# Order at the entry of a two-layer transformer kernel, the place of four small loads, and the last output tile in two halves

## The chip, the cores and the metric

The kernel runs on one core of a Trainium2 chip. The metric is the time of one execution on the device in microseconds (us). Five engines work side by side and wait for each other through semaphores: TensorE (PE in the profile, its weight loads as PEld), VectorE (DVE), ScalarE (ACT), GpSimd (POOL), and SyncE (SP), whose queue issues nearly all DMA transfers.

## The reference

The program computes a two-layer block over 512 latent tokens and 256 context tokens of width 1024. Each layer is an attention mixer and a SwiGLU feed-forward part; both take normalised tokens that are scaled and shifted by a modulation computed from a conditioning vector, and both are gated by it. Layer 0 mixes with windowed and dense grouped-query attention, layer 1 with differential attention, in which a scalar lambda weighs two softmaxes.

```python
s_c, s_cc = silu(c), silu(c_ctx)
for l in range(2):
    mx, mc = s_c @ mod_w[l] + mod_b[l], s_cc @ mod_w[l] + mod_b[l]
    shx1, scx1, gx1, shx2, scx2, gx2 = split(mx, 6)           # mc likewise
    hx = rms(x, norm_mix_w[l]) * (1 + scx1) + shx1            # hc likewise
    if l == 0:
        q, k, v (groups A and B) = hx @ ev_w_in, hc @ ev_w_in # then norms, rotary, attention
    else:
        lam = exp(sum(lq1 * lk1)) - exp(sum(lq2 * lk2)) + lam_init
        a = softmax(q1 k1) - lam * softmax(q2 k2)             # then values, norm, projection
    x = x + gx1 * mixed
    x = x + gx2 * (silu(gate) * up) @ ffn_w_out[l]            # gate, up from ffn_w_in[l]
    ...                                                       # ctx likewise in layer 0
return x
```

## The kernel before

Products that need full precision are made from halves: an operand is cast to a rounded float (`hi`) on ACT, the rest (`lo`) is subtracted on DVE or POOL, and three matmuls (hi by hi, hi by lo, lo by hi) add up in one PSUM bank.

**Entry.** Tokens lie in six tiles of 128 (four latent, two context, in the order `CTX_FIRST`). `start_mod(n)` makes two chunks of the modulation, shift (part 0) and scale (part 1), for 256 of the 1024 columns: `mod_steps` loads each chunk in two pieces of 512 KB (L177), multiplies them with the conditioning vector (L182), copies the row out of PSUM on ACT (`modr`, L185), turns it into columns with four small matmuls (`modcol`, L191), and `add_mod` adds the bias (L276) and, for the scale, the norm's weight (L280). Between these calls the tokens are normalised and transposed. Then, for each of the eight column blocks, DVE scales and shifts the transposed tokens (`xT`, L1165), ACT casts them (L1170) and DVE or POOL subtracts (L1171), into `hT` and `hTc`.

**First in-projection.** `weights0(0, ...)` loads the weights of the first head group in four pieces of 256 rows, three transfers each (`wir`, L493), casts each piece on ACT (`wihi`, L500) and subtracts on DVE (`wilo`, L501). The raw pieces share a ring of six buffers with the modulation's pieces (`start_tile`, tag `mw`), so a weight piece takes the buffer of a modulation piece that PE has used. In program order the loads of pieces 0 and 1 stand first, then the casts of 0 and 1, then the load and the cast of 2, then those of 3. `in_proj0` then sums 24 matmuls for each token tile (L466 to L468), two of the eight column blocks at a time.

**Order.** The program is traced in Python, and a planner orders each engine's queue by a simulated timeline: an instruction may move ahead of others that were written before it if its inputs are there sooner. From the sixth attention step on PE's own order is taken as written. `behind(name)` adds edges: what the block traces on the engine of the instruction kept in `turn[name]` is queued behind that instruction.

**Lambda.** `lambda_rows` makes four loads of 64 numbers each, one number per partition (L632). It is called in the second pass of layer 0's way out (`way_out0`), from the hook after the ninth hidden slice, `small_loads`. Its tile's pool is open from the start.

**Way out of layer 1.** `way_out1` holds eight PSUM banks, one for each pair of token tile and half row (512 columns). The last four hidden slices are held back: for one bank after the other, twelve matmuls finish the sum, `residual` multiplies by the gate (L473, in place in PSUM) and adds to the tokens (L474), and the 256 KB are stored (L1091).

Of the kernel before, what the change touches and what calls it, by code (L numbers as in the profile page):

```python
# [19 lines left out]
P = 128  # L20
# [9 lines left out]
NF = FFN // P  # L30
# [33 lines left out]
def backbone(es: ExitStack, tc: tile.TileContext, x, c, ctx, c_ctx, mod_w, mod_b, norm_mix_w, norm_ffn_w,  # L64
# [12 lines left out]
    turn = {"acc": 0, "tr": 0, "sum": 0}  # L77
# [12 lines left out]
    def raw_tile(shape, name):  # L90
        return keep.tile(shape, F32, name=name, tag="raw", bufs=2)
# [30 lines left out]
    start = Pool("start")  # L122
# [45 lines left out]
    def mod_steps(l, part, n, new_tile, pool, bank, wide=None, room=("modr", 1)):  # L168

        width, pieces = 256, 2  # L170
        c0 = part * D + n * width
        ps = p_1.tile([P, width], F32, name="mod", tag=bank) if wide is None else \
            wide.pool.tile([P, 1024], F32, name="mod", tag="sc", bufs=2)[:, :width]
        kp = KT // pieces
        for pc in range(pieces):
            w = new_tile([P, kp, width], "modw")
            nc.sync.dma_start(  # L177
                w, mod_w[l, pc * kp * P:(pc + 1) * kp * P, c0:c0 + width].rearrange("(j p) n -> p j n", p=P))
            for a in range(kp):
                k = pc * kp + a  # L180
                j = k % 4
                nc.tensor.matmul(ps[32 * j:32 * j + 32, :], s_pad[:, k, :], w[:, a, :],  # L182
                                 start=k < 4, stop=k >= 4, tile_position=(0, 32 * j))
        r = pool.tile([P, width], F32, name="modr", tag=room[0], bufs=room[1])
        nc.scalar.copy(r, ps)  # L185
        yield
        nb = width // P
        k0, k1 = n * nb, (n + 1) * nb
        pc2 = p_1.tile([P, nb, 2], F32, name="modcol", tag=bank)
        for b in range(nb):  # L190
            nc.tensor.matmul(pc2[:, b, :], r[:, b * P:(b + 1) * P], sel2, start=True, stop=True)  # L191
        add_mod(l, part, k0, k1, pc2, 2)
# [80 lines left out]
    def add_mod(l, part, k0, k1, ps, streams):  # L273

        mc = modc[l][:, part, k0:k1, 0:streams]
        nc.vector.tensor_tensor(mc, ps, bc(bcol[:, l, part, k0:k1], 2, streams), ALU.add)  # L276
        if part in (1, 4):
            f = 0 if part == 1 else 1
            w0 = 16 + 16 * f + 8 * l
            nc.vector.scalar_tensor_tensor(aff[l][:, f, k0:k1, 0:streams], mc, 1.0,  # L280
                                           bc(cols[:, w0 + k0:w0 + k1], 2, streams), ALU.add, ALU.mult)
# [198 lines left out]
        return hi, lo  # L480


    def weights0(b, wp, subs, new_tile=raw_tile):

        qc, kc, vc = ((b * 256, 512 + 64 * b, 640 + 64 * b) if b < 2 else
                      (768 + (b - 2) * 256, 1280 + 64 * (b - 2), 1408 + 64 * (b - 2)))
        for u in range(4):
            if u in (0, 2, 3):
                raws = []
                for v in ((0, 1), None, (2,), (3,))[u]:  # L490
                    raws.append(new_tile([P, 2, 384], "wir"))
                    for c0, c1, s in ((0, 256, qc), (256, 320, kc), (320, 384, vc)):
                        turn["load"] = nc.sync.dma_start(  # L493
                            raws[-1][:, :, c0:c1],
                            ev_w_in[0, v * 256:(v + 1) * 256, s:s + c1 - c0].rearrange("(j p) n -> p j n", p=P))
                if not u:
                    yield
            raw = raws.pop(0)
            hi, lo = (wp.tile([P, 2, 384], F32R, name=f"wi{z}", tag=f"w{z}", bufs=WBUF + 1) for z in ("hi", "lo"))
            nc.scalar.copy(hi, raw)  # L500
            subs[u % len(subs)].tensor_sub(lo, raw, f32(hi))  # L501
            yield hi, lo
# [125 lines left out]
    def lambda_rows(mp):  # L628

        lqk = mp.tile([HD, 4], F32, name="lqk")  # L630
        for j, a in enumerate((od_lq1, od_lk1, od_lq2, od_lk2)):
            nc.sync.dma_start(lqk[:, j:j + 1], a.rearrange("o d -> d o"))  # L632
        return lqk
# [415 lines left out]
    def way_out1(xs, hidr, pool, places_w, places_h):  # L1049

        banks = [p_1.tile([P, 512], F32, name="dps", tag=tag) for tag in ("tr0", "tr1", "acc0", "acc1")]
        banks += [singles.pool.tile([P, 512], F32, name="dps", tag=tag, bufs=2) for tag in ("p0", "p0", "p1", "p1")]
        places = [(t, n) for t in range(NTX) for n in range(2)]
        held = 4
        ready = {}

        def ready_hid(f):
            def views(raw):
                yield raw, ffn_w_out[1, f * P:(f + 1) * P, :]
            if f < len(places_w):  # L1060
                raw = raw_tile([P, D], "wdr")
                turn["load"] = nc.sync.dma_start(raw, ffn_w_out[1, f * P:(f + 1) * P, :])
                w, h = places_w[f], places_h[f]
                split_into(w, raw.rearrange("p (k c) -> p k c", k=4))
                split_into(h, hidr[f].rearrange("p (k c) -> p k c", k=2))
            else:
                w = [z.rearrange("p (k c) -> p k c", k=4) for z in unit(pool, views, [P, D], 5, "wd")]
                h = [pool.tile([P, 2, SEQ // 2], F32R, name=name, tag=name, bufs=5) for name in ("hdh", "hdl")]
                split_into(h, hidr[f].rearrange("p (k c) -> p k c", k=2))
            ready[f] = h, w  # L1070

        def sums(f, i):
            (t, n), ps = places[i], banks[i]
            hh, hl = (z[:, t // 2, t % 2 * P:(t % 2 + 1) * P] for z in ready[f][0])
            a, b = (z[:, 2 * n:2 * n + 2, :] for z in ready[f][1])
            nc.tensor.matmul(ps, hh, a, start=f == 0, stop=False)  # L1076
            nc.tensor.matmul(ps, hh, b, start=False, stop=False)  # L1077
            nc.tensor.matmul(ps, hl, a, start=False, stop=f == NF - 1)  # L1078

        g = gate_row(1, 5, 0, pool)  # L1080
        for f in range(NF - held):
            ready_hid(f)
            for i in range(len(places)):
                sums(f, i)
        for f in range(NF - held, NF):
            ready_hid(f)
        for i, (t, n) in enumerate(places):
            for f in range(NF - held, NF):
                sums(f, i)
            residual(xs[t], banks[i], g, n)  # L1090
            nc.sync.dma_start(out[0, t * P:(t + 1) * P, n * 512:(n + 1) * 512], xs[t][:, n * 512:(n + 1) * 512])  # L1091

    class Pairs:

# [50 lines left out]
    wp = Pool("mw0", "right")  # L1145
    xs = {t: load_x(t) for t in CTX_FIRST[:2]}
# [25 lines left out]


    mods = [(0, part, n) for part in (2, 3, 4) for n in range(4)]
    ws = list(weights0(0, wp.pool, (nc.vector,), start_tile))[1:]
    tabs = {}
    tables0(0, tabs, wp.pool)

# [66 lines left out]
    units = weights0(1, wp.pool, (nc.gpsimd, nc.vector))  # L1245
    next(units)
    ws = [next(units) for _ in range(2)]
    if True:
        for i, (b, t) in enumerate(steps):
            j = i % NT  # L1250
# [7 lines left out]
            if j == 4 and b < 2:  # L1258
                units = weights0(b + 2, wp.pool, (nc.gpsimd, nc.vector))
                next(units)  # L1260
            if b < 3:
                n = QUARTS[b][j]
# [13 lines left out]
                if j == 4 and b < 2:  # L1276
                    ws = [next(units) for _ in range(2)]
# [10 lines left out]
            if t == 0:  # L1288
# [13 lines left out]
                wp = Pool("w0", "right")  # L1302
                opa = Pool("opa", "right")
                xs = [None] * NT
                units = out_units0(wp.pool)
                ws = [next(units)]
# [36 lines left out]
        i = len(steps) - 1  # L1343
# [112 lines left out]
    if True:  # L1456
# [33 lines left out]
        places = [(rows[a], [z[:, a].rearrange("p (t c) -> p t c", c=P) for z in t2]) for a in range(4)]  # L1490
        raws = [f32(z)[:, 4 * half:5 * half].rearrange("p (t c) -> p t c", c=P) for z in rows4]
# [9 lines left out]
        ws1 = []  # L1501

        def small_loads():
            ws1.append(lambda_rows(cp))

        def early_weight(u):
            def room(shape, name):
# [13 lines left out]
    wp = Pool("mw1", "right")  # L1521
# [44 lines left out]
    if True:  # L1566
        new_head(ws1)
        first = state[0]
        banks = {t: acc_tile("inps") for t in CTX_FIRST[:2]}
# [34 lines left out]
        xs = xs1  # L1604
# [16 lines left out]
        ws, raws = [], []  # L1621
# [8 lines left out]
        for i in range(last - 1):  # L1630
# [14 lines left out]
            elif i in (23, 24):  # L1645
                z = keep.tile([P, 2, D], F32R, name="wo", tag=f"hTc{i - 23}")
# [37 lines left out]
        wp = Pool("w1", "right")  # L1684
# [203 lines left out]
```

## Time and profile before

| | |
|---|---|
| time, three runs | 1695.99 us median, 1693.12 to 1697.33 |
| profiled execution | 1692.5 us, span 1690.7 us |
| granted TensorE clock, mean | 0.995 |
| busy share of the span | PE 96%, PEld 87%, DVE 68%, ACT 56%, POOL 41% |
| HBM | 179.92 MB read, 12.87 MB written, 114 GB/s |

The span is the time from the first to the last instruction of the program; the execution's time has 1.8 us around it. A row of a timeline reads: start, length, engine, line of the kernel, operation, what it writes and reads, shapes, how many in a row, and in brackets the engine's idle time before it and what ended it. An engine name with a q is its sequencer: SPq rows are DMA issues. A row of a window table reads: stretch, length, busy time and count of PE, PEld, DVE, ACT and POOL, granted clock, share of the 16 DMA engines, GB/s. A row of waits reads: total, times, longest.

### The profile page before, as it was taken

Reading aid. Unit: us, or ns where it says so; the run is one execution under the profiler, and the core shown is the slowest. Engines: PE = TensorE matmul, PEld = TensorE weight load, DVE = VectorE, ACT = ScalarE, POOL = GpSimd, SP = SyncE. Lnnn points to the kernel's source line nnn. Section 1 sums busy time; section 2 is a strip of 40 time slices with the busy share of each in tenths; the row PEclk is TensorE's granted clock in tenths of the full one; section 3 lists DMA queues with packets and bytes.
Section 4 is the critical chain, followed back from the end, with each engine's and each line's share of the span. In section 5 each row is a group of like instructions: output and inputs, shape, how many; then the busy total and the mean of one; then the engine's idle time right before and its main releaser. Section 6 shows DMA issues by size and latency. Waiting matters only on the chain. (4 is left out here: it accounts for less than half of the span.)

```text
span 1690.7 us, 28553 instructions
## 1 busy us (share of the span) xinstructions
PE 1628.1 (96%) x10378; PEld 1465.3 (87%) x10378; DVE 1143.5 (68%) x2012; ACT 938.4 (56%) x2011; POOL 695.1 (41%) x867
## 2 busy tenths in 40 slices
PE   6999999899999999999999989999999999999998
PEld 3877777677999999998877889999988899999887
DVE  3765656754799887767767656666666598887433
ACT  5565555745456665544664456666666555555321
POOL 2665554321445554412413366666665242221000
PEclk9999999999999999999999999999999999999999
DMA  9222221411455555439966311111112433331431
GB/s 315 75 71 71 73 70 51 173 52 39 134 162 174 165 158 161 135 107 348 307 184 184 98 42 38 47 45 43 46 47 101 124 94 103 108 103 57 137 99 63
DMA packets 217964, 194.64 MB, mean 115 GB/s; under 512 B 20000, under 2 KB 202592, under 8 KB 217824
## 3 DMA queue, kind: packets, MB, share of 16 engines
q1 hardware_dynamic: 217472, 192.62, 36.9%
q8 instruction: 81, 1.33, 0.3%
q14 instruction: 59, 0.48, 0.1%
q10 hardware_dynamic: 352, 0.21, 0.0%
HBM read 179.92 MB, written 12.87 MB: 114 GB/s over the span
## 5 line engine op out<-in xcount | busy, mean ns | idle before, releaser
L901 ACT CAST wbh<-wr 128x512 fp32r<-128x512 f32 x170 | 104.9, 621 | 139.4 <-PE p L933 78.6
L933 PE MATMUL p<-hT,wbh 128*128 128x256 f32 (+1 forms) x752 | 154.4, 299 | 0.0
L911 POOL TENSOR_TENSOR wbl<-wr,wbh 128x512 fp32r<-128x512 f32 x43 | 60.2, 1400 | 174.2 <-ACT wbh L901 174.2
L933 PEld LDWEIGHTS p<-hT,wbh 128*128 128x128 f32 x752 | 121.9, 191 | 0.2
L911 DVE TENSOR_TENSOR wbl<-wr,wbh 128x512 fp32r<-128x512 f32 x127 | 106.4, 847 | 22.2 <-ACT wbh L901 17.8
L933 PE MATMUL p<-hT,wbl 128*128 128x256 f32 (+1 forms) x376 | 111.9, 298 | 0.0
L933 PE MATMUL p<-t,wbh 128*128 128x384 f32 (+1 forms) x480 | 111.3, 318 | 0.0
L604 POOL TENSOR_SCALAR Pt<-Pt,rc 128x256 f32<-128x256 f32 (+3 forms) x96 | 73.1, 772 | 86.9 <-DVE rc L601 79.6
L231 POOL TENSOR_TENSOR modp<-modp 128x512 f32<-128x512 f32 x40 | 57.3, 1433 | 116.5 <-ACT modp L230 116.5
L933 PE MATMUL p<-hTt,wbh 128*128 128x256 f32 (+1 forms) x480 | 101.0, 303 | 0.0
L466 PE MATMUL inps<-wih,hT 128*128 128x384 f32 x256 | 90.0, 351 | 7.2 <-ACT qkv L677 7.2
L887 POOL TENSOR_TENSOR wr<-wr 128x512 f32<-128x512 f32 x40 | 61.6, 1541 | 84.3 <-DVE ws L892 81.9
L933 PE MATMUL p<-b,wbh 128*128 128x384 f32 x368 | 93.8, 336 | 0.4 <-DVE c L961 0.4
L901 ACT CAST wbh<-ws 128x512 fp32r<-128x512 f32 x120 | 69.3, 579 | 42.1 <-PE p L933 31.0
L224 DVE SCALAR_TENSOR_TENSOR ma<-modw,cols,ma 128x256 f32<-128x256 f32 x140 | 87.0, 621 | 2.3
L592 ACT ACTIVATE Pt<-sc,nm 128x256 f32<-128x256 f32 (+3 forms) x96 | 67.8, 708 | 34.8 <-DVE nm L588 18.8
L468 PE MATMUL inps<-wih,hT 128*128 128x384 f32 x256 | 86.1, 336 | 0.0
L467 PE MATMUL inps<-wil,hT 128*128 128x384 f32 x256 | 86.0, 336 | 0.0
L911 DVE TENSOR_TENSOR wbl<-ws,wbh 128x512 fp32r<-128x512 f32 x120 | 81.8, 681 | 2.1 <-ACT wbh L901 2.0
L933 PEld LDWEIGHTS p<-t,wbh 128*128 128x128 f32 x480 | 82.9, 189 | 0.0
L933 PEld LDWEIGHTS p<-hTt,wbh 128*128 128x128 f32 x480 | 78.3, 191 | 3.1 <-ACT modp L230 2.1
L230 ACT ACTIVATE modp<-modw,cols 128x256 f32<-128x256 f32 x160 | 68.3, 499 | 17.1 <-POOL ma L236 8.6
(355 smaller groups left out, 5357.4 us busy)
## 6 DMA issues: line engine op xcount, KB each, us to landing
modw<-in_mod_w_dram SPq DMA_DIRECT2D x96, 512.0 KB, 4.4
wr<-in_ffn_w_in_dram SPq DMA_DIRECT2D x176, 256.0 KB, 3.1
wdr<-in_ffn_w_out_dram SPq DMA_DIRECT2D x66, 512.0 KB, 3.7
wir<-in_od_w_in_dram SPq DMA_DIRECT2D x96, 128.0 KB, 2.3
hidm<-hid SPq DMA_DIRECT2D x44, 192.0 KB, 1.9
hr<-hidm SPq DMA_DIRECT2D x22, 192.0 KB, 3.1
x<-in_x_dram SPq DMA_DIRECT2D x8, 512.0 KB, 6.2
wir<-in_ev_w_in_dram SPq DMA_DIRECT2D x16, 256.0 KB
```

The source lines that it names most:

```text
L224: nc.vector.scalar_tensor_tensor(acc, w[:, k], scale[k], acc, ALU.mult, ALU.add)
L230: nc.scalar.activation(pr[:, k], w[:, k], AF.Copy, scale=scale[k])
L231: nc.gpsimd.tensor_add(pr[:, 0:2], pr[:, 0:2], pr[:, 2:4])
L466: nc.tensor.matmul(ps, hs[0][:, k, :], a, start=k == 0, stop=False)
L467: nc.tensor.matmul(ps, hs[0][:, k, :], b, start=False, stop=False)
L468: nc.tensor.matmul(ps, hs[1][:, k, :], a, start=False, stop=k == KT - 1)
L592: turn["exp"] = nc.scalar.activation(p[:, :n], s, AF.Exp, bias=nm[:, c1], accum_out=sm[:, c1])
L604: nc.gpsimd.tensor_scalar(p[:, :n], p[:, :n], rc[:, hh:hh + 1], 1.0, ALU.mult, ALU.mult)
L887: nc.gpsimd.tensor_sub(w, raw[f, "G1"], w)
L901: nc.scalar.copy(hi, w)
L911: (nc.gpsimd if name == "G2" else nc.vector).tensor_sub(lo, raw[need[n]], f32(hi))
L933: nc.tensor.matmul(ps, w[:, k, :], H[b][h][:, k, :], start=first and k == 0 and q == 0, stop=final and k == 3 and q == 2, skip_group_check ...
```

## The change

- `mod_steps` keeps its latest row copy in `turn["modr"]`.
- `weights0` takes a list of which pieces are loaded at which step; the other callers keep the old one. The entry calls it so that all four pieces are loaded in the first step, and traces the four casts inside `behind("modr")`: on ACT they are queued behind the last row copy of `start_mod(3)`.
- `small_loads` traces the lambda loads inside `behind("load")`: on SP they are queued behind the weight load of the way out that was traced last.
- `way_out1` takes its last bank (token tile 3, columns 512 to 1023) in two halves of 256 columns: twelve matmuls, multiply, add and store for the first half, then the same for the second. Both halves are slices of the same PSUM bank.

```diff
         r = pool.tile([P, width], F32, name="modr", tag=room[0], bufs=room[1])
-        nc.scalar.copy(r, ps)
+        turn["modr"] = nc.scalar.copy(r, ps)
...
-    def weights0(b, wp, subs, new_tile=raw_tile):
+    def weights0(b, wp, subs, new_tile=raw_tile, loads=((0, 1), (), (2,), (3,))):
...
-            if u in (0, 2, 3):
+            if not u:
                 raws = []
-                for v in ((0, 1), None, (2,), (3,))[u]:
...
+            for v in loads[u]:
+                raws.append(new_tile([P, 2, 384], "wir"))
+                for c0, c1, s in ((0, 256, qc), (256, 320, kc), (320, 384, vc)):
+                    turn["load"] = nc.sync.dma_start(
...
+            if not u:
+                yield
...
-        for i, (t, n) in enumerate(places):
+        for i, (t, n) in enumerate(places[:-1]):
             for f in range(NF - held, NF):
                 sums(f, i)
             residual(xs[t], banks[i], g, n)
             nc.sync.dma_start(out[0, t * P:(t + 1) * P, n * 512:(n + 1) * 512], xs[t][:, n * 512:(n + 1) * 512])
+        t, n = places[-1]
+        for c in range(2):
+            ps, cs = banks[-1][:, c * 256:(c + 1) * 256], slice(n * 512 + c * 256, n * 512 + (c + 1) * 256)
+            for f in range(NF - held, NF):
+                hh, hl = (z[:, t // 2, t % 2 * P:(t % 2 + 1) * P] for z in ready[f][0])
+                a, b = (z[:, 2 * n + c, :] for z in ready[f][1])
+                nc.tensor.matmul(ps, hh, a, start=False, stop=False, skip_group_check=True)
+                nc.tensor.matmul(ps, hh, b, start=False, stop=False, skip_group_check=True)
+                nc.tensor.matmul(ps, hl, a, start=False, stop=f == NF - 1, skip_group_check=True)
+            nc.vector.tensor_mul(ps, ps, g[:, cs])
+            nc.vector.tensor_add(xs[t][:, cs], xs[t][:, cs], ps)
+            nc.sync.dma_start(out[0, t * P:(t + 1) * P, cs], xs[t][:, cs])
...
-    ws = list(weights0(0, wp.pool, (nc.vector,), start_tile))[1:]
+    units = weights0(0, wp.pool, (nc.vector,), start_tile, ((0, 1, 2, 3), (), (), ()))
+    next(units)
+    with behind("modr"):
+        ws = list(units)
...
         def small_loads():
-            ws1.append(lambda_rows(cp))
+            with behind("load"):
+                ws1.append(lambda_rows(cp))
```

More of the change, by code (lines that the diff above doesn't have):

```diff
@@ L487, in weights0 @@
         for u in range(4):
-            if u in (0, 2, 3):
+            if not u:
                 raws = []
-                for v in ((0, 1), None, (2,), (3,))[u]:
[L491 to L497, printed above, removed]
+            for v in loads[u]:
+                raws.append(new_tile([P, 2, 384], "wir"))
+                for c0, c1, s in ((0, 256, qc), (256, 320, kc), (320, 384, vc)):
+                    turn["load"] = nc.sync.dma_start(
+                        raws[-1][:, :, c0:c1],
+                        ev_w_in[0, v * 256:(v + 1) * 256, s:s + c1 - c0].rearrange("(j p) n -> p j n", p=P))
+            if not u:
+                yield
             raw = raws.pop(0)
@@ L1075, in sums @@
             a, b = (z[:, 2 * n:2 * n + 2, :] for z in ready[f][1])
-            nc.tensor.matmul(ps, hh, a, start=f == 0, stop=False)
-            nc.tensor.matmul(ps, hh, b, start=False, stop=False)
-            nc.tensor.matmul(ps, hl, a, start=False, stop=f == NF - 1)
+            nc.tensor.matmul(ps, hh, a, start=f == 0, stop=False, skip_group_check=True)
+            nc.tensor.matmul(ps, hh, b, start=False, stop=False, skip_group_check=True)
+            nc.tensor.matmul(ps, hl, a, start=False, stop=f == NF - 1, skip_group_check=True)
         g = gate_row(1, 5, 0, pool)
@@ L1091, in way_out1 @@
             nc.sync.dma_start(out[0, t * P:(t + 1) * P, n * 512:(n + 1) * 512], xs[t][:, n * 512:(n + 1) * 512])
+        t, n = places[-1]
[5 more added lines that the diff above has]
+                nc.tensor.matmul(ps, hh, a, start=False, stop=False, skip_group_check=True)
+                nc.tensor.matmul(ps, hh, b, start=False, stop=False, skip_group_check=True)
+                nc.tensor.matmul(ps, hl, a, start=False, stop=f == NF - 1, skip_group_check=True)
+            nc.vector.tensor_mul(ps, ps, g[:, cs])
+            nc.vector.tensor_add(xs[t][:, cs], xs[t][:, cs], ps)
+            nc.sync.dma_start(out[0, t * P:(t + 1) * P, cs], xs[t][:, cs])
     class Pairs:
```

## The prediction

> **What bounds the kernel now.** I read the page first, then the clock and transfer windows of the first 60 us, then the timelines of SP, ACT, DVE and PE there, and last the timeline of the final 8 us.
>
> ```profile
> span 1690.7 us, 28553 instructions
> PE 1628.1 (96%) x10378; PEld 1465.3 (87%) x10378; DVE 1143.5 (68%) x2012; ACT 938.4 (56%) x2011; POOL 695.1 (41%) x867
> ```
>
> TensorE is busy for 96% of the span, so only what PE does not do, or does at a lower clock, can be won. The change touches three places: the entry, up to the first in-projection sums; the second pass of layer 0's way out, where the lambda rows are now loaded; and the last output tile. SP's queue in the entry:
>
> ```profile
> 22.69 1.24 SPq L632 DMA_DIRECT2D lqk<-in_od_lq_dram  x1
> 25.95 0.47 SPq L632 DMA_DIRECT2D lqk<-in_od_lk_dram  x1
> 27.60 2.93 SPq L177 DMA_DIRECT2D modw<-in_mod_w_dram  x5
> ...
> 28.00:29.00 1.00, 1.00 (x10) 0.20 (x8) 0.07 (x1) 0.70 (x2) 0.00 (x0) 0.50 0.48 71
> 29.00:30.00 1.00, 1.00 (x8) 0.71 (x5) 0.00 (x0) 0.37 (x1) 0.00 (x0) 0.60 0.80 236
> ```
>
> The last three numbers of a window are granted clock, DMA share and GB/s. The four lambda loads, a few hundred bytes each, stand on SP between 22.69 and 26.42, ahead of the last five pieces of modulation weight. Two microseconds later the transfer engines run dry, the only two slices with a share under 0.9 between 3 and 40 us. Next ACT, the engine that makes the weights' casts and copies the modulation rows out of PSUM:
>
> ```profile
> 40.42 0.83 ACT L500 CAST wihi<-wir 128x768 fp32r<-128x768 f32 x1 [2.72 <-DMA wir<-in_ev_w_in_dram]
> 41.15 0.36 ACT L185 COPY modr<-mod 128x256 f32<-128x256 f32 x1
> 41.60 1.80 ACT L500 CAST wihi<-wir 128x768 fp32r<-128x768 f32 x2
> 44.33 0.36 ACT L185 COPY modr<-mod 128x256 f32<-128x256 f32 x1
> ```
>
> ACT stands idle for 2.72 us in front of a cast whose weights have not landed, with two row copies queued behind it. DVE does the same with the cast's low half:
>
> ```profile
> 38.39 0.16 DVE L276 TENSOR_TENSOR modc<-modcol,bcol 128x4 f32<-128x4 f32 x1 [1.00 <-PE modcol L191]
> 41.28 0.96 DVE L501 TENSOR_TENSOR wilo<-wir,wihi 128x768 fp32r<-128x768 f32 x1 [2.73 <-ACT wihi L500]
> 42.16 0.15 DVE L280 SCALAR_TENSOR_TENSOR aff<-modc,cols 128x4 f32<-128x4 f32 x1
> 42.35 1.65 DVE L1165 TENSOR_SCALAR xT<-xT,aff,modc 128x256 f32<-128x256 f32 x4
> 50.98 0.97 DVE L280 SCALAR_TENSOR_TENSOR aff<-modc,cols 128x4 f32<-128x4 f32 x1
> ```
>
> What PE makes of it:
>
> ```profile
> 38.28 1.37 PE L182 MATMUL mod<-modw,s_pad 128*32 128x256 f32 x16
> 41.57 0.61 PE L191 MATMUL modcol<-cst,modr 128*128 128x2 f32 x4 [1.92 <-ACT modr L185]
> 42.29 0.44 PE L467 MATMUL inps<-wilo,hTc 128*128 128x384 f32 x1
> 42.92 0.34 PE L467 MATMUL inps<-wilo,hTc 128*128 128x384 f32 x1
> 43.10 0.34 PE L468 MATMUL inps<-wihi,hTc 128*128 128x384 f32 x1
> 44.92 0.69 PE L467 MATMUL inps<-wilo,hTc 128*128 128x384 f32 x1 [1.29 <-DVE wilo L501]
> 47.64 0.52 PE L466 MATMUL inps<-wihi,hT 128*128 128x384 f32 x1
> 47.96 0.52 PE L467 MATMUL inps<-wilo,hT 128*128 128x384 f32 x1
> ...
> PE inps L466 <- ACT qkv L520: 1.4, 2, 1.1
> ...
> 43.00:44.00 1.00, 0.63 (x4) 0.29 (x2) 1.00 (x4) 1.00 (x3) 0.00 (x0) 0.72 1.10 243
> 50.00:51.00 1.00, 1.00 (x8) 1.00 (x7) 0.41 (x3) 0.00 (x0) 1.00 (x1) 0.86 0.76 223
> ```
>
> PE loses time three times. It has nothing from 39.65 (38.28 and 1.37) to 41.57; it waits 1.29 us for the second low half until 44.92; and it then starts a sum every 0.32 us (47.64, 47.96) instead of every 0.18 us (42.92, 43.10). The two windows give the granted clock 0.72 and 0.86: at half clock from about 43.4 to 50.3. The row between them is from the waits of 58 to 130 us: twice, 1.4 us together, PE stood for ACT's copy of finished sums.
>
> **Part by part, the lambda rows.** Without the four loads the remaining pieces of modulation weight can be issued as their buffers come free, so the dry slices close: 0.52 and 0.20 of a microsecond by their shares. Bounds: nothing (if a buffer rather than the queue's place holds the pieces) and 3.7 us (the whole time from 22.69 to 26.42); I take 0.7, the idle share itself. Everything that lands behind moves by it: PE's last modulation piece ends at 38.95, the first cast starts at 39.7.
>
> In their new place the four issues cost SP up to the same 3.7 us, behind the weight load of the ninth hidden slice in the second pass. It falls in about this stretch, and the reader of the rows is far away:
>
> ```profile
> 884.00:892.00 8.00, 8.00 (x41) 6.68 (x41) 4.31 (x10) 4.31 (x9) 1.29 (x1) 1.00 0.50 139
> L641 PE MATMUL lps<-lpr,cst x2: 247/258/268, 998.4 to 998.5; 64*128 64x2 f32 x2
> ```
>
> PE has no idle time there and the transfers are at half load, so I take 0. What hides it is the load that is issued ahead; with that cover gone, the slice's sums would be up to 3.7 us late.
>
> **The casts behind the row copy.** All twelve loads of the first weights are now written ahead of the casts (four of the pieces' buffers are those of modulation pieces, as before), and ACT may start no cast before the last row copy. Nothing is added; what moves is the copies. The last one, now at 44.33, can run when its piece is summed: 39.0 to 39.4. Its columns then take PE 0.6 us, to 40.0. The copy from 41.15 fits into ACT's idle time, and the shift and scale (42.16, 42.35: 0.15 and 1.65 us) into DVE's 2.73. The first cast still starts with its transfer: 39.7 to 40.5, its low half 40.55 to 41.5; the second cast follows to 41.4, its low half from 41.5 to 42.45. So PE can start its low-half sums at 41.55 instead of 42.29, and goes on with the second pair at 42.5, where it now waits until 44.92: 2.4 us earlier, the 0.7 above included. Behind the casts, on ACT, stand only the casts of the tokens' last columns; their readers on PE have the sums of six token tiles over the first columns ahead of them. Bounds: 0.7 (only the transfers move) and 3.8 (the first tile is finished early as well, and the 1.4 us for ACT's copies go). I take 2.4.
>
> **The clock.** From 44.92 to 50.2 PE runs at 0.32 a sum where 0.175 would do: 5.3 x (1 - 0.175/0.32) = 2.4 us. The stretch before the drop and the one before that, with an earlier one for the rivals:
>
> ```profile
> 20.00:30.00 10.00, 8.34 (x52) 5.91 (x53) 5.06 (x10) 7.51 (x15) 3.46 (x7) 0.66 1.01 306
> ...
> 36.60:40.05 3.45, 2.41 (x32) 0.95 (x24) 0.95 (x3) 0.37 (x1) 0.17 (x1) 1.00 1.12 294
> 40.05:43.46 3.41, 1.89 (x11) 1.63 (x11) 2.14 (x6) 2.84 (x5) 0.00 (x0) 1.00 0.80 214
> ```
>
> The first number after the length is PE's busy time: after 2.41 us in the second row the clock stayed full, after 1.89 in the third it was halved. In the changed kernel the second stretch would hold some 2.5 us of PE's work. Bounds 0 and 2.4; I take 2.4, as 2.5 lies by the row that kept the clock.
> [...]
>
> **The last tile.** Rows for its price:
>
> ```profile
> 1369.15 1.44 PE pz L933 x12
> 1683.37 0.39 PE L1076 MATMUL dps<-wdh,hdh 128*128 128x512 f32 x1
> 1687.03 0.69 DVE L474 TENSOR_TENSOR x<-x,dps 128x512 f32<-128x512 f32 x1
> 1685.02 3.05 SPq L1091 DMA_DIRECT2D out_dram<-x  x2
> DMA to landing us min/median/max: 2.0/2.0/2.0
> L961 DVE TENSOR_TENSOR p<-p,s x20: 418/433/433, 1374.8 to 1564.4; 128x256 f32<-128x256 f32 x20
> PE dps L1030 <- DVE x L474: 1.5, 3, 1.0
> ```
>
> The first row, from the chain of waits, is twelve sums of 256 columns; the one from the source's answer is an add of 256 columns in PSUM.
> Now: twelve sums of 512 columns from 1683.37, multiply and add to 1687.72 (1687.03 and 0.69), store, landed 2.0 later at 1689.75. Then: twelve sums of 256 columns take 1.44 (and 0.16 for the last to drain): 1684.97. Multiply and add of 256 columns in PSUM take 0.433 each, 0.9 together: 1685.9. If the second half's sums run meanwhile, PE ends at 1686.4, DVE at 1687.35: 0.4 us better. If they wait until the add has let go of the bank, they run from 1685.9 to 1687.5, DVE to 1688.45, landed at 1690.45: 0.7 us worse. The nearest row is the last: PE's sums wait for the add on a bank, so I take +0.7. The smaller store may land a little sooner; I give it nothing.
> [...]
>
> **Sum.** -2.4 (entry, 0.7 of it the lambda rows) - 2.4 (clock) + 0.7 (tail) = -4.1 us. The profiled execution took 1692.5 us (span 1690.7), so one like it would take 1688.4; the median of the runs shown, 1695.99, is 3.5 higher, and I forecast against it: 1691.9. A measurement of this kernel can tell about 0.3%, 5.1 us, from no change: below 1690.9 is faster, above 1701.1 slower.
>
> **Rivals.** First, the clock drops all the same, at another place: -2.4 + 0.7 = -1.7, 1694.3. For it: the slice from 20 to 30 us, at clock 0.66 with PE busy for 8.34 of 10 us. Against: PE has no wait left in the stretch to 43.4.
> Second, nothing but transfers counts: the cast waited for its DMA already (2.72 us), and if the dry slices merely move, PE starts as before: 0 + 0.7, 1696.7.
> Third, more than forecast. The first token tile is finished early, because its last columns no longer come at 50.98, so its rotation overlaps PE's other tiles and the wait for the qkv copies (1.4) goes. With it and with halves that overlap, -4.1 - 1.4 - 1.1 = -6.6, 1689.4.
> Fourth, slower. The casts are held behind the row copy, and the program's order on ACT and DVE is made by a planner, not by the edit. If it leaves the copy where it stands, behind the casts of the tokens (44.33), the four weight casts go behind it: the first at 44.7 instead of 40.42, 4.3 us later, with PE idle long enough for the low clock to last half as long again (3.4 us of the 6.9 that it lasted, at half speed: 1.7). 4.3 + 1.7 + 0.7 = 6.7, 1702.7. It decides if the copy runs later than the first weights land, 40.4. For it: the planner put the copies behind a cast that wasn't ready. Against: the piece is summed by 39.65, before the weights land.
>
> **Chances.** Forecast 0.40 (0.12 of it with enough of the third rival's wait to pass 5.1 us), first rival 0.20, second 0.06, third 0.22, fourth 0.12. So faster 0.34, within 0.3% 0.54, slower 0.12. The range goes from a little under the third rival's 1689.4, as its parts may be larger and runs scatter by 2 us around the median, to the second rival and the same scatter: 1686.5 to 1698.5.
>
> **What would show it.** Right: no lambda load before 800 us and no DMA share under 0.9 between 26 and 36 us; the last row copy before the first weight cast, near 39; the first low-half sum by 41.6 and no wait for the second; sums 0.175 apart from 42 to 50; PE waiting about 0.9 us between the halves of the last tile. Wrong: a first cast after 41; a granted clock under 0.9 in the slices from 43 to 50; the two halves back to back; and, for all of it, gains at 60 us that are gone again at 120, or a PE wait of over 1 us in a place that the change does not touch.

## The result, and the profile after

The changed kernel takes 1698.68 us (median, 1694.84 to 1702.35), the kernel before 1696.16 in the same comparison (1692.85 to 1699.39): ratio 1.0014, 95% interval 1.0007 to 1.0020. By that interval it is slower, by 2.4 us (1.2 to 3.4), where 4.1 less was forecast; how far a single ratio can be trusted is measured below. The profiled execution took 1699.0 us. Its page begins:

```profile
span 1697.2 us, 28578 instructions
PE 1633.3 (96%) x10390; PEld 1468.7 (87%) x10390; DVE 1144.0 (67%) x2014; ACT 938.1 (55%) x2011; POOL 697.6 (41%) x867
```

PE is busy 5 us longer for the same sums (1633.3 instead of 1628.1), and the span is 6.5 longer, more than the medians differ. The entry, first the windows (length; PE, PEld, DVE, ACT, POOL; then granted clock, DMA share, GB/s), then ACT's, DVE's and PE's timelines (line numbers behind the edits are shifted by 12 to 16):

```profile
28.00:30.00 2.00, 2.00 (x28) 1.51 (x20) 0.66 (x4) 1.80 (x4) 0.00 (x0) 1.00 1.10 349
34.00:36.00 2.00, 2.00 (x20) 1.29 (x23) 1.91 (x3) 0.15 (x1) 1.30 (x1) 0.50 1.10 349
50.00:51.00 1.00, 1.00 (x8) 1.00 (x7) 1.00 (x4) 0.36 (x1) 0.00 (x1) 1.00 0.00 0
```

```profile
39.07 0.37 ACT L185 COPY modr<-mod 128x256 f32<-128x256 f32 x1 [1.16 <-PE modcol L191]
40.31 0.62 ACT L1182 CAST hT<-xT 128x512 fp32r<-128x512 f32 x1 [0.87 <-DVE xT L1177]
...
41.88 0.37 ACT L185 COPY modr<-mod 128x256 f32<-128x256 f32 x1
42.14 2.30 ACT L500 CAST wihi<-wir 128x768 fp32r<-128x768 f32 x3
```

```profile
43.27 0.41 DVE L390 TENSOR_TENSOR rt<-rp,rw 128x256 f32<-128x256 f32 x1
...
44.61 0.95 DVE L501 TENSOR_TENSOR wilo<-wir,wihi 128x768 fp32r<-128x768 f32 x1
45.55 1.81 DVE L501 TENSOR_TENSOR wilo<-wir,wihi 128x768 fp32r<-128x768 f32 x2
```

```profile
34.63 2.79 PE L182 MATMUL mod<-modw,s_pad 128*32 128x256 f32 x24
...
38.91 1.93 PE L182 MATMUL mod<-modw,s_pad 128*32 128x256 f32 x16
...
45.61 0.69 PE L467 MATMUL inps<-wilo,hTc 128*128 128x384 f32 x1 [1.12 <-DVE wilo L501]
46.09 0.52 PE L468 MATMUL inps<-wihi,hTc 128*128 128x384 f32 x1
46.41 0.52 PE L466 MATMUL inps<-wihi,hTc 128*128 128x384 f32 x1
```

The dry slices are gone (DMA share 1.10 between 28 and 30, where it was 0.48 and 0.80). But the last row copy runs at 41.88, not at 39.0 to 39.4, the first weight cast at 42.14 instead of 40.42, and DVE makes rope tables (43.27) before the first low half. PE's first low-half sum comes at 45.61; before it was 42.29. And PE's clock is at half from 32.45 to 49.51: sums 0.32 apart, and the last pieces of the modulation in 2.79 and 1.93 us instead of 1.50 and 1.37.

That isn't where the time is lost for good, though. The first token tile is finished earlier than before (its copy at 55.68 instead of 58.93), and PE's waits between 50 and 140 us show the third rival's gain (the wait for ACT's copy falls from 1.4 to 0.6) and a new loss beside it:

```profile
PE ppt L612 <- POOL Pt L604: 2.2, 3, 1.4
PE inps L466 <- ACT qkv L520: 0.6, 2, 0.5
```

The wait of 1.4 us is in the fifth attention step, 85 us behind the edit. PE before, from the step's last eight transposes to the next projection sum, then the same after:

```profile
131.14 0.56 PE L612 MATMUL ppt<-cst,Pt 128*128 128x128 f32 x3
132.14 0.77 PE L612 MATMUL ppt<-cst,Pt 128*128 128x128 f32 x5 [0.45 <-POOL Pt L604]
...
133.27 0.42 PE L466 MATMUL inps<-wihi,hT 128*128 128x384 f32 x1
```

```profile
130.67 0.44 PE L612 MATMUL ppt<-cst,Pt 128*128 128x128 f32 x2
132.52 0.33 PE L612 MATMUL ppt<-cst,Pt 128*128 128x128 f32 x1 [1.42 <-POOL Pt L604]
133.30 0.76 PE L612 MATMUL ppt<-cst,Pt 128*128 128x128 f32 x5 [0.45 <-POOL Pt L604]
...
134.42 0.42 PE L466 MATMUL inps<-wihi,hT 128*128 128x384 f32 x1
```

PE reaches the transposes 0.47 us earlier than before, and the next projection sum 1.15 later: 3.75 us instead of 2.13. What it waits for is POOL's division of the attention weights by their sum. POOL and ACT, before and after:

```profile
130.51 1.58 POOL L604 TENSOR_SCALAR Pt<-Pt,rc 128x640 f32<-128x640 f32 x2 [1.44 <-DVE rc L601]
```

```profile
129.62 0.19 ACT L598 ACTIVATE es<-es 128x2 f32<-128x2 f32 x1
```

```profile
130.66 0.69 POOL L530 TENSOR_TENSOR kd<-qy,kd 128x128 fp32r<-128x128 f32 x1 [2.46 <-issue]
131.67 1.57 POOL L604 TENSOR_SCALAR Pt<-Pt,rc 128x640 f32<-128x640 f32 x2 [0.32 <-DVE rc L601]
```

```profile
129.91 0.42 ACT L525 CAST qd<-qy 128x256 fp32r<-128x256 f32 x1
130.22 0.31 ACT L529 CAST kd<-qy 128x128 fp32r<-128x128 f32 x1
130.42 0.22 ACT L598 ACTIVATE es<-es 128x2 f32<-128x2 f32 x1
```

The sum needs `es`, a small exponential of the sink. Before, ACT makes it as soon as the step's own exponentials are done (129.62). After, two casts for the next projection stand ahead of it on ACT (129.91, 130.22), and it comes at 130.42; DVE's sum and reciprocal and POOL's division follow 1.2 us later than before. Nobody edited these lines. The planner orders ACT, DVE and POOL by its simulated timeline, and PE too up to the sixth step; with the entry moved it laid all four out differently from the first token tiles to here.

The loss at this step stays: matched instruction by instruction, PE lies 1.16 us behind the first profile right after it and 1.05 at 190 us. The rest of the 6.5 us between the two profiles came later: some 1.5 and 1.9 us where the clock was halved at 199.70 and 923.33, 1.5 between 835 and 850 us, where PE waits 1.07 us for DVE at 849.81 (the first profile lacks this wait, but the unchanged program has it in its second profile, n1_same below, 1.08 us), and the last tile's 0.5.

The tail, PE and DVE:

```profile
1691.94 0.39 PE L1098 MATMUL dps<-wdh,hdh 128*128 128x256 f32 x1 [0.98 <-DVE x L1102]
```

```profile
1694.14 0.42 DVE L1102 TENSOR_TENSOR x<-x,dps 128x256 f32<-128x256 f32 x1
```

The halves run one behind the other, with the wait of 0.98 (forecast: about 0.9). From the end of the last full bank's add (the seventh of the eight banks) to the end of the span it was 5.72 us before (1684.99 to 1690.71) and is 6.20 now (1690.99 to 1697.19): +0.48.

### The profile page after: what moved, and what is told of

The parts are those of the page before. It is cut to its first block, busy times and chain, and to the rows that moved or that the text cites. A ratio compares the mean times of both kernels' runs of the same rounds, so it can differ in the third digit from the quotient of the medians.

```text
span 1697.2 us, 28578 instructions
## 1 busy us (share of the span) xinstructions
PE 1633.3 (96%) x10390; PEld 1468.7 (87%) x10390; DVE 1144.0 (67%) x2014; ACT 938.1 (55%) x2011; POOL 697.6 (41%) x867
```

## The experiments

The theory tested: the queueing of four casts at the entry makes the planner choose another order up to the sixth attention step, and the loss is the wait at 131 us in that order. Rivals: the entry's own late sums (fourth rival of the prediction), the clock, the lambda rows' new place, the tail.

The table gathers what the experiments below gave. "Reached" is when PE starts the last eight transposes of the fifth step, "took" the time from there to the next projection sum (in the rows above 131.14 and 2.13 before, 130.67 and 3.75 after), "half clock" how long PE's clock was halved in the first 60 us.

| kernel | queueing | ratio to before (95%) | reached | took | half clock |
|---|---|---|---|---|---|
| before (first profile) | no | 1 | 131.14 | 2.13 | 13.65 |
| n1_same | no | 0.9998 (0.9986, 1.0010) | 130.99 | 2.12 | 13.65 |
| f3_loads_alone | no | 1.0000 (0.9988, 1.0013) | 130.35 | 2.13 | 20.48 |
| e3_tail | no | 1.0024 (1.0012, 1.0035) | 132.95 | 2.12 | 20.48 |
| e5_tail_again | no | 0.9999 (0.9987, 1.0011) | 131.16 | 2.12 | 17.07 |
| e11_tail_sbuf | no | one run | 132.19 | 2.12 | 20.48 |
| e2_lambda | no | 0.9999 (0.9985, 1.0013) | 130.83 | 2.12 | 13.65 |
| e7_free_no_tail | no | 0.9994 (0.9984, 1.0003) | 130.34 | 2.12 | 13.65 |
| e4_free | no | 1.0004 (0.9995, 1.0013) | 129.28 | 2.12 | 13.65 |
| after | yes | 1.0014 (1.0007, 1.0020) | 130.67 | 3.75 | 17.07 |
| e1_entry | yes | 1.0037 (1.0024, 1.0050) | 132.54 | 4.06 | 20.48 |
| f2_queue_alone | yes | 1.0008 (0.9996, 1.0019) | 131.58 | 4.27 | 17.07 |
| e6_no_tail | yes | 1.0014 (1.0001, 1.0026) | 132.06 | 4.72 | 17.07 |
| e8_mend | yes, mended at 130 us | 1.0006 (0.9995, 1.0016) | 129.65 | 2.91 | 10.24 |
| e9_mend_no_tail | yes, mended at 130 us | 0.9999 (0.9987, 1.0010) | 130.02 | 2.90 | 10.24 |
| e10_tables_late | yes, tables moved | 1.0007 (0.9994, 1.0020) | 132.93 | 2.71 | 13.65 |

### The parts one by one

**n1_same**, the kernel before, unchanged.

> The kernel before, unchanged, as one of the kernels compared: how far two sets of runs of one program differ. Chance theory (PE's clock is halved in stretches of 3.41 us whose places vary from one execution to the next): the profile shows the same instructions in the same order with halved stretches at other places than 22.97 and 43.45 us, and PE up to 5 us apart from the first profile; ratio 1.0000, within 0.0010. Order theory: the drops belong to the order of the instructions, so they come at 23 and 43 us again.

Measured 0.9998. Its own profile has a span of 1694.1 us, 3.4 more than the first profile of the same program, and the clock is halved at other places: 33.45 to 47.10, 81.24, 197.29 and 859.5 us instead of 22.97 and 43.45. Windows of 3.41 us, each followed by the next, of n1_same and then of the first profile:

```profile
193.88:197.29 3.41, 0.88 (x8) 0.61 (x6) 2.98 (x2) 2.47 (x7) 2.44 (x3) 1.00 0.16 44
197.29:200.70 3.41, 3.41 (x15) 2.79 (x16) 1.75 (x4) 0.52 (x2) 1.33 (x2) 0.50 0.79 259
```

```profile
193.63:197.04 3.41, 1.60 (x11) 1.32 (x10) 2.40 (x2) 2.37 (x6) 2.57 (x3) 1.00 0.03 6
197.04:200.45 3.41, 2.69 (x20) 2.37 (x21) 2.60 (x6) 1.26 (x5) 1.06 (x2) 1.00 0.81 246
```

The same stall of PE near 195 us falls whole into one window in the one execution (0.88 us of work) and is shared between two in the other (1.60): the clock halves in the first and not in the second. So the clock of one profile doesn't belong to the program.

**e1_entry**, the entry's edit alone; **e2_lambda**, the lambda rows alone; **e3_tail** and **e5_tail_again**, the last tile alone. Each is the kernel before with only that part of the diff.

> The entry's edit alone (all loads of the first weights ahead, their casts behind the row copy); lambda loads and last tile as before. Order theory: the planner puts the last row copy near 42 behind casts of the tokens, so the first weight cast starts at 41.5 to 42.5 instead of 40.4 and the first low half leaves DVE near 45.5, behind four rope tables; PE is 1 to 1.5 us later than before at 132 us, ratio 1.0007 (1.0003 to 1.0012). Chance theory (the edit is neutral, and what differs is where the clock was halved): PE within 0.4 us of before once the halved stretches are taken off, ratio 0.9995 to 1.0003.

> The lambda rows alone are moved; entry and last tile as before. Order theory: the transfers close up, the first weights land about 1 us earlier (39.3 instead of 40.34), the first low-half sum comes at 41.3 to 41.6 instead of 42.29; ratio 0.9995 (0.999 to 0.9998). Lambda theory (the four issues hold up the second pass): a PE wait of over 1 us between 840 and 930 that before lacks, ratio 1.0005 to 1.0012. Own reading: between 860 and 930 nothing changes by more than 0.3 us beside a halved clock.

> The last tile's two halves alone. PE waits 0.98 us between the halves as in the changed kernel, DVE's last add ends 0.8 us later against PE's last full bank, and the smaller store gives 0.3 back: +0.5 us, ratio 1.0003 (1.0000 to 1.0006). Rival: the store is what ends the program, and a store of half the size brings it even, +0.0.

> The last tile's two halves alone, once more, since 4 us had been measured for an edit whose own rows show 0.5. Chance theory: the same 0.5 in the last tile and another sum of halved stretches, ratio 1.0003 to 1.0010. Rival (the edit costs 3 us before the last tile, in each execution): ratio 1.002 again, with the same waits at the same places as in the first run of it.

The entry alone: 1.0037, more than the 1.0012 that was expected at most; last row copy at 42.60, first weight cast at 42.87, first low-half sum at 46.90. Between the transposes and the next projection sum it takes 4.06 us. The lambda rows alone: 0.9999, with the first weight cast at 39.38 as expected, but the first low-half sum at 43.03 instead of 41.3 to 41.6, with PE's clock halved from 33.22 to 46.87. At their new place they cost nothing that shows: PE's sums at 860 and at 908 us stand equally far (1.03 us) from those of before. SP there, in the changed kernel:

```profile
880.26 0.56 SPq L632 DMA_DIRECT2D lqk<-in_od_lq_dram  x1
...
882.14 0.60 SPq L632 DMA_DIRECT2D lqk<-in_od_lk_dram  x1
883.85 0.33 SPq L1014 DMA_DIRECT2D hr<-hidm  x1
```

The tail alone was measured twice: 1.0024, then 0.9999. Up to the last tile its instructions stand in the order of before on every engine, and in both profiles the tail costs the same 0.48 us (6.20 from the last full bank's add to the end). What made the rest of the first result isn't shown: the halved stretches up to the last tile sum to 30.7 us in the first profile and to the same 30.7 in the second. The two comparisons were made on different chips, each against the kernel before on its own, so the chip is not excluded either. A cost ahead of the last tile in each execution is out; but two comparisons of one program can differ by 0.0025, so differences of 0.001 between kernels are not read from a single ratio here, and the changed kernel's 1.0014 isn't either. What speaks for a real loss is that the four kernels with the queueing, and nothing else moved behind it, all lie above 1 (1.0008 to 1.0037), while of the seven without it all but e3_tail lie between 0.9994 and 1.0004. The column "took" varies by 0.01 us among kernels with one order while the clock is full, and can be read.

**e4_free** and **e7_free_no_tail**: loads ahead and lambda rows late, without the queueing; e7 with the last tile as before. **e6_no_tail**: the changed kernel with the last tile as before.

```diff
     next(units)
-    with behind("modr"):
-        ws = list(units)
+    ws = list(units)
```

> As the changed kernel, but the casts are not held behind the row copy; all four pieces are still loaded ahead. Order theory: the casts start when the weights land, 39.3 to 40.5, between the row copies; the first low-half sum at 42.0 to 42.6 instead of 45.6; ratio to before 0.9998 to 1.0003, that is 2 us better than the changed kernel. Chance theory: as the changed kernel, 1.0014. Third possibility, that it is the loads' new place that costs and not the queueing: also 1.001 or more, with the first weights landing after 40.

> All loads of the first weights ahead and the lambda rows late, without the queueing behind the row copy, and the last tile as before. Order theory: first low-half sum near 42 or earlier, PE 1.9 us earlier than before at 132 us as in the kernel with the tail, nothing given back at the end: ratio 0.9989 (0.998 to 0.9997), the best so far. Chance theory: 1.0000, within 0.0010.

> The changed kernel with the last tile as before: casts behind the row copy, all loads ahead, lambda rows late. Order theory: the entry's 1 to 2 us are left, ratio 1.0008 (1.0003 to 1.0014), first low-half sum after 44. Chance theory: ratio 0.9990 to 1.0005. If the tail costs more than its 0.5: ratio under 1.000.

1.0004, 0.9994, and 1.0014. The first low-half sums of e4 and e7 come at 42.74 and 42.52, and PE is 0.80 us ahead of before in e7 at the fifth step, where 1.9 was expected. Without the queueing the wait of 1.42 is gone (2.12), with it and without the tail it stays (a wait of 1.43 in 4.72 us, in part at half clock). ACT in e7_free_no_tail:

```profile
38.94 0.83 ACT L500 CAST wihi<-wir 128x768 fp32r<-128x768 f32 x1 [0.63 <-DMA wir<-in_ev_w_in_dram]
39.68 0.37 ACT L185 COPY modr<-mod 128x256 f32<-128x256 f32 x1
40.49 0.83 ACT L500 CAST wihi<-wir 128x768 fp32r<-128x768 f32 x1 [0.44 <-DMA wir<-in_ev_w_in_dram]
```

Casts and copies interleave, and the first cast waits 0.63 us for its transfer instead of 2.72: ACT's idle time that the change was to use is gone once the lambda loads are out of the way. e7's 0.9994 is the lowest ratio of all, but its interval holds 1; that it beats the kernel before isn't shown.

**f2_queue_alone** and **f3_loads_alone** split the entry's edit.

```diff
-    units = weights0(0, wp.pool, (nc.vector,), start_tile, ((0, 1, 2, 3), (), (), ()))
+    units = weights0(0, wp.pool, (nc.vector,), start_tile)
```

is f2 against e1; f3 is e1 without `behind("modr")`.

> Of the entry's edit the queueing alone: the four casts behind the row copy, the loads written in the old order; lambda rows and last tile as before. Theory: the queueing by itself makes the later order, so the wait of 1.4 us on POOL's division near 131 us is there, the first low-half sum comes after 44, ratio 1.0008 to 1.0025. Rival (loads and queueing together do it): no wait over 0.6 near 131, ratio 0.999 to 1.0005.

> Of the entry's edit the loads alone: all four pieces written ahead of the casts, no queueing; lambda rows and last tile as before. Theory: SP issues them in the order in which it issued them before, so nothing changes: waits of 1.4 on ACT's copy and two of 0.5 on POOL's division between 58 and 135 us as before, ratio 1.0000 within 0.0010. Rival: the loads ahead are what costs, ratio 1.001 or more.

The loads written ahead change nothing: SP issues in its old order, ratio 1.0000, took 2.13. The queueing alone has it all: last row copy at 42.76, first low-half sum at 46.49, the wait of 1.42 at 133.44 and a halved clock from 134.72; took 4.27. Its 1.0008 and e1's 1.0037 belong to programs with one order on every engine, which shows the scatter again; these two were also measured on different chips.

### The order at 130 us put back

**e8_mend**: the changed kernel, and at this one step `es` ahead of the two casts, its sum and reciprocal ahead of the next maximum, the division ahead of a subtraction. **e9_mend_no_tail**: the same with the last tile as before.

```diff
+            first = ("es",) if b == 1 and t == CTX_FIRST[4] else ()
+            with behind(*first):
+                nc.scalar.copy(qd[:, :, 0, :], y[:, 0:4])
...
+            with behind(*(("div",) if first else ())):
+                nc.gpsimd.tensor_sub(kd[:, 1], kb, f32(kd[:, 0]))
...
+                    with behind(*(("rc",) if (b, t, hp, hh) == (0, 3, 0, 0) else ())):
+                        nc.vector.tensor_reduce(mx, s, AX.X, ALU.max)
```

> The changed kernel, with the order near 130 us put back by hand on ACT, DVE and POOL: the exponential of the sink (L598 before) ahead of two casts for the next projection, its sum and reciprocal ahead of the next maximum, the division of the weights (L604) ahead of a subtraction; PE's order is unchanged. Theory (the queueing at the entry makes the planner lay out the steps up to 132 us in another order, in which the division comes 1.2 us later and PE waits 1.42 us for it): the division starts at 130.3 to 130.7 on the changed kernel's scale instead of 131.67, the wait is 0.5 or less, PE at 136 us about 1.1 us earlier than in the changed kernel against its place at 128 us, ratio 1.0004 (0.9998 to 1.0010). Rival (the casts' later start at the entry is what costs, whatever happens at 130): ratio 1.0014 again.

> The same mended order, and the last tile as before. Theory: 0.5 us less than the kernel with the halves, so about as the kernel before, ratio 1.0000 (0.9993 to 1.0007); the wait at 131 us is again 0.5 or less. Rival: 1.0010.

ACT, POOL and PE of e8_mend (lines shifted by 5):

```profile
128.90 0.22 ACT L603 ACTIVATE es<-es 128x2 f32<-128x2 f32 x1
```

```profile
129.69 1.70 POOL L609 TENSOR_SCALAR Pt<-Pt,rc 128x640 f32<-128x640 f32 x2 [2.50 <-ACT kd L532]
```

```profile
129.65 0.44 PE L617 MATMUL ppt<-cst,Pt 128*128 128x128 f32 x2
130.66 0.33 PE L617 MATMUL ppt<-cst,Pt 128*128 128x128 f32 x1 [0.57 <-POOL Pt L609]
...
132.56 0.42 PE L466 MATMUL inps<-wihi,hT 128*128 128x384 f32 x1
```

The wait falls from 1.42 to 0.57 (0.5 or less expected), "took" from 3.75 to 2.91 (0.84; 1.1 expected), and the ratios are 1.0006 and 0.9999. So at full clock 0.84 of the 1.62 us that the step takes longer is the order of these few instructions, and for this half the theory stands in the trace; the times alone agree with it but could not carry it. The other 0.78 us goes with the queueing too (no kernel without it takes more than 2.13), but this run leaves the order ahead of the step as it is, and no run takes that part back. Both profiles have the shortest half-clock stretch at the entry (10.24 us), with the entry's program unchanged.

### The entry's first sums

**e10_tables_late**: DVE's rope tables behind the low half of the second weight piece, last tile as before.

```diff
+            low = subs[u % len(subs)].tensor_sub(lo, raw, f32(hi))
+            if u == 1:
+                turn["low"] = low
...
+    with behind("low"):
+        tables0(0, tabs, wp.pool)
```

> The changed kernel with the last tile as before and with DVE's four rope tables queued behind the low half of the second weight piece, so that DVE makes the first low half right after its cast. First low-half sum 1.0 to 1.6 us earlier against the first weight cast than in the changed kernel (there 45.61 for a cast at 42.14). Theory (the planner's order up to 132 us decides, not the entry's own microseconds): the order changes once more, and the time goes where the waits between 60 and 135 us go, anywhere from 0.9992 to 1.0015; PE's waits in that stretch sum to the same as the lag. Rival (the entry's first sums decide): 1 us better than without the tables' move, ratio 1.0004 or less.

ACT, DVE and PE:

```profile
41.49 2.30 ACT L500 CAST wihi<-wir 128x768 fp32r<-128x768 f32 x3
```

```profile
42.62 0.95 DVE L501 TENSOR_TENSOR wilo<-wir,wihi 128x768 fp32r<-128x768 f32 x1
```

```profile
43.62 0.68 PE L467 MATMUL inps<-wilo,hTc 128*128 128x384 f32 x1
```

From the first cast to the first low-half sum it takes 2.13 us instead of 3.47, as expected: 1.34 us won at the entry. At the fifth step nothing is left of it: reached 132.93, 0.87 later than e6_no_tail, whose clock was halved just as long up to there (17.07 us). The order is a third one (took 2.71). The rival that the entry's first sums decide gets no support from this; but as the order behind changed as well, and the ratio of 1.0007 (0.9994 to 1.0020) holds the rival's 1.0004, it isn't excluded.

### The tail

**e11_tail_sbuf**: the last tile alone, with the product in SBUF.

```diff
-            nc.vector.tensor_mul(ps, ps, g[:, cs])
-            nc.vector.tensor_add(xs[t][:, cs], xs[t][:, cs], ps)
+            prod = pool.tile([P, 256], F32, name="prod", tag="prod", bufs=2)
+            nc.vector.tensor_mul(prod, ps, g[:, cs])
+            nc.vector.tensor_add(xs[t][:, cs], xs[t][:, cs], prod)
```

> The last tile's two halves alone, with the product written to SBUF instead of back into the bank, so that the bank is let go after the multiply. If PE's second half waits for DVE's last access to the bank, the wait falls from 0.98 to 0.5 (one operation of 0.43 less) and the program ends 0.4 to 0.5 us earlier after the last full bank than with the product in the bank. If it is the store or the number of operations that counts, nothing changes.

```profile
1690.24 0.39 PE L1098 MATMUL dps<-wdh,hdh 128*128 128x256 f32 x1 [0.52 <-DVE prod L1102]
```

The wait falls from 0.98 to 0.52, and from the last full bank's add to the end it takes 5.74 us instead of 6.20: with the bank let go one operation earlier the halves cost nothing against before (5.72), and still gain nothing.

## Why the prediction was wrong, point by point

**The lambda rows** (-0.7): right, and rather under-sized. Among the kernels without queueing, the first weight cast starts at 40.42, 39.75, 39.41, 41.17, 40.69 and 40.31 in six profiles with the lambda loads at the entry (mean 40.3) and at 39.38, 38.94 and 39.22 in the three without them (39.2): 1.1 us earlier, though the two groups all but touch and their clocks differ. The new place costs 0, as said.

**The casts behind the row copy** (-2.4): here the prediction failed. Its step was that the last copy "can run when its piece is summed: 39.0 to 39.4". The piece was summed at 40.84, because PE ran at half clock, and the planner left three casts of the tokens ahead of the copy, until 41.88. That is the fourth rival's mechanism, past the point (40.4) that it named; it was given 0.12. The next step, that the low half follows its cast at once, failed too: DVE had four rope tables in between. The sum came out 3.3 us later, not 0.7 earlier.

The second of the two costs more, and does so whatever the clock does. e9_mend_no_tail has the same order at the entry, and its clock was full from 20 us up to 39.41:

```profile
39.41 0.36 ACT L185 COPY modr<-mod 128x256 f32<-128x256 f32 x1
39.67 2.44 ACT L500 CAST wihi<-wir 128x768 fp32r<-128x768 f32 x3
41.86 0.42 DVE L390 TENSOR_TENSOR rt<-rp,rw 128x256 f32<-128x256 f32 x1 [0.98 <-DMA rp<-in_rope_dram]
43.21 0.95 DVE L501 TENSOR_TENSOR wilo<-wir,wihi 128x768 fp32r<-128x768 f32 x1
```

There the piece was summed at 38.38. The copy ran 1.03 us behind that, after its three casts (1.04 in the changed kernel), but the copy and the first cast came when the prediction said (39.0 to 39.4 and 39.7). Still the first low half starts 3.54 us behind its cast, and the first low-half sum comes at 44.22. In all six kernels with the queueing and the tables in their place that distance is 2.47 to 3.54 us, where it was 0.86 before.

But this loss isn't the result either. By the fifth attention step most of it has been made up: the six kernels with the queueing reach the transposes at 131.1 us on average (129.65 to 132.54), the nine without at 131.0 (129.28 to 132.95). The averages flatter the queueing, as the clock of the six was halved for less time up to there (15.4 us against 18.2); among the seven with 17.07 us it is 131.4 against 130.8, where two executions of one order (after and e6_no_tail) are 1.4 apart. So a part of the loss may remain. The first tile's early end and the shorter wait for ACT's copies, the third rival's mechanism, gave the other part back. What the prediction had in no step is the order behind the entry: it treated the edit as a move inside 39 to 45 us. Its last sentence named the sign ("a PE wait of over 1 us in a place that the change does not touch"), without a price. The price is 1.62 us at full clock (3.75 instead of 2.13), and 1.9 to 2.6 in the other three kernels with that order, whose clock was halved at the wait's end or right behind it, from 133.8, 134.7 and 135.9 us:

```profile
132.51:135.92 3.41, 1.53 (x12) 1.08 (x11) 0.93 (x5) 1.53 (x4) 2.27 (x3) 1.00 0.00 0
135.92:139.33 3.41, 3.41 (x17) 3.22 (x16) 1.87 (x5) 1.08 (x4) 0.21 (x2) 0.50 0.00 0
```

These are windows of e1_entry: the wait leaves 1.53 us of PE's work in one window, and the next runs at 0.50.

**The clock** (-2.4): the term belongs to no edit. The step was that the change would fill "the second stretch", as if the windows lay at 36.60, 40.05 and 43.46 in each execution. They don't: in n1_same, the same program, the clock is halved from 33.45 to 47.10, and among the nine profiles without queueing the halved time in the first 60 us is 13.65 to 20.48, among the six with it and without the tables' move 10.24 to 20.48. The length of a wait doesn't tell the place either: in the first profile PE waited 1.92 us up to 41.57, ahead of the drop at 43.45, and 2.19 us (for a transfer, L182) up to 34.59, behind which the clock stayed full. The 2.4 us should have been left out and put into the range.

**The tail** (+0.7): +0.48. The mechanism was right: PE waits 0.98 us for DVE's add on the bank. DVE ends 0.85 later (2.72 us behind the last full bank's add before, 3.57 after; 0.73 forecast), and the smaller store, which was given nothing, lands 0.37 sooner (3.00 us from DVE's end to the span's end before, 2.63 after).

**The sum.** The rows shown give +1.6 to +2.6 for the wait, +0.5 for the tail and about -1 for the transfers: +1.1 to +2.1, against a measured 2.4 (1.2 to 3.4). Of the wait, 0.84 has been taken back by an experiment; the rest of the sum is read from rows. How much of the transfers' 1.1 us reaches the end isn't settled: the kernels with the lambda rows moved and no queueing reach the fifth step at 130.2 on average, those without the move at 131.5, but their halved stretches differ too.

## What to carry to other kernels

Where a planner orders the queues, an edge at one place is a new order for everything behind it that isn't fixed by hand: price such an edit by the first place where the order is pinned, and compare the waits up to there, not the edited stretch alone. A time inside one profile that hangs on the clock should be looked at in a second profile of the same program before it becomes a term of a sum. And where single ratios scatter by 0.002, the same few instructions' distance, which repeats to 0.01 us while the clock is full, is the better measure.

## What the runs showed of the hardware

In the 16 profiles the halved stretches of the first 60 us sum to multiples of 3.41 us (10.24, 13.65, 17.07 and 20.48 in the table), and within a profile their starts lie whole numbers of 3.413 us apart: 6 in the first profile (22.97 and 43.45 us), 49 and 261 in the changed kernel's (32.45, then 199.70 and 923.33), 14, 48 and 242 in that of n1_same (33.45, then 81.24, 197.29 and 859.5). I laid a grid of such windows through each of the 16 profiles, by the start of its halved stretches, from 20 to 1680 us. Of the windows at full clock, all 21 with under 1.55 us of PE busy time were followed by a halved one, 27 of 159 with 1.55 to 2.40, and none of 7474 with more. The window of e1_entry shown above, from 132.51 us, is one of the 21: 1.53 us of work, with a longest wait of 1.43, and the next window at 0.50. The grid's place against the program's start differs from execution to execution: one program has a window from 193.63 us in the first profile and from 193.88 in n1_same.
